# A rotary-embedding kernel: nine transfers on one queue instead of ten, in another order

## The chip, the cores and the metric

One core of a Trainium2 chip runs the kernel. The metric is the device time of one execution in microseconds (us). A profile's span is about 1.7 us shorter than that time (160.1 against 161.85 us in the profiled execution of the kernel before); points in time below count from the start of the span, unless kernel times are meant.

## The reference

The input x is fp32 of shape (16, 512, 16, 64), 33.5 MB. The first 32 of each 64 values are rotated with cosine and sine; the other 32 are copied.

```python
def reference(x, cos, sin):          # cut to what matters; h = 16
    a, b = x[..., 0:16], x[..., 16:32]
    first  = a * cos[..., :16] - b * sin[..., :16]
    second = a * sin[..., :16] + b * cos[..., :16]
    return concatenate([first, second, x[..., 32:]], axis=-1)
```

Every byte of x must come in once and go out once, 67.1 MB in all.

## The kernel before

The data are four tiles of 128 partitions x 64 KB. A partition's part of a tile is 16 rows of 4 KB. Three tiles fit into a ring in SBUF, an on-chip memory, so tile 3 takes the place of tile 0 and cannot be loaded before tile 0 has been stored. All loads and stores are issued by SP (SyncE), on one hardware queue, in program order; VectorE does all arithmetic, in place.

```python
# ... (NS = 3 slots, K = 16 rows, KC = 8, K0 = 4, T = 4 tiles)
    def load(t, lo=0, hi=K):
        nc.sync.dma_start(out=rows(t, lo, hi), in_=xf[t, :, lo * R : hi * R])

    def store(t, lo=0, hi=K):
        nc.sync.dma_start(out=of[t, :, lo * R : hi * R], in_=rows(t, lo, hi))

    nc.gpsimd.dma_start(out=stage[:, 0]..., in_=cosf)      # cut
    nc.gpsimd.dma_start(out=stage[:, 1]..., in_=sinf)      # cut
    load(0, 0, K0)
    load(0, K0, K)
    load(1)
    load(2, 0, KC)
    # ... four VectorE copies spread the tables over 128 partitions
    def rotate(t, lo, hi):
        # ... x1 = first halves of rows lo to hi of tile t; c, s = tables; b_t in PSUM (on-chip too)
        nc.vector.tensor_mul(out=b_t, in0=x1, in1=s)
        nc.vector.tensor_mul(out=x1, in0=x1, in1=c)
        nc.vector.tensor_sub(...)
        nc.vector.tensor_add(...)

    rotate(0, 0, K0)
    rotate(0, K0, (K0 + K) // 2)
    rotate(0, (K0 + K) // 2, K)
    store(0)
    load(2, KC, K)
    load(3)
    for t in range(1, T):
        rotate(t, 0, KC)
        rotate(t, KC, K)
        store(t)
```

So the queue carries: load 0 in 4 and 12 rows, load 1, the first half of load 2, store 0, the second half of load 2, load 3, stores 1, 2, 3. The half load behind store 0 has a purpose: load 3 waits for store 0 to land, and the half load keeps the queue busy meanwhile.

## Time and profile before

| | before |
|---|---|
| kernel time, median of the first 3 runs | 161.82 us (161.75 to 162.03) |
| span of the profiled execution | 160.1 us |
| VectorE (DVE) busy | 110.0 us |
| queue q1, share of 16 engines' span | 97.8% |

From the page of the kernel before: busy time; VectorE's and the DMA engines' share of each of 40 slices, in tenths; the hardware queue (packets, MB, share of the 16 engines' span); and the chain that ended last, by engine (from the last instruction back to what released it, step by step; a q after an engine's name is the part of it that issues and waits).

```profile
DVE 110.0 (69%) x40; POOL 1.3 (1%) x6
...
DVE  0069709999999999999999994799999900000000
...
DMA  6999999699699799899996996996996996996991
...
q1 hardware_dynamic: 1440, 67.11, 97.8%
...
DMA 50%; DVE 28%; DVEq 1%; issue 0%; SPq 0%
```

The row of DMA digits looks ragged (6, 9, 9, 6, ...), but a packet counts in the slice in which it starts, and a 64 KB packet takes 2.4 us against a slice of 4.0 us. The share in the queue's line, 97.8%, is the reading that matters. The trace also keeps a record of each packet: the queue's add up to 156.49 us per engine, and only 156.85 us lie between the first one's start (1.75) and the last one's end (158.60). A 64 KB packet takes 2.418 us in the median, so 16 engines move 16 x 65536 B / 2.418 us = 434 GB/s.

The timeline of the kernel before (start and duration in us; engine, line, operation; output from input; in brackets the idle time before it). SPq lines are issues of transfers; several are merged, with the time from the first issue to the end of the last.

```profile
0.74 1.88 SPq L53 DMA_DIRECT2D ring<-in_x_dram  x4
...
11.94 2.30 DVE L83 TENSOR_TENSOR b_t<-ring,table 128x2048 f32<-128x2048 f32 x1
...
44.14 0.35 SPq L56 DMA_DIRECT2D out_dram<-ring  x1
...
44.53 28.14 SPq L53 DMA_DIRECT2D ring<-in_x_dram  x2
...
72.77 55.64 SPq L56 DMA_DIRECT2D out_dram<-ring  x3
...
125.77 2.28 DVE L88 TENSOR_TENSOR ring<-ring,b_t 128x2048 f32<-128x2048 f32 x1
```

Store 0 is issued at 44.14, while the half load ahead of it in the queue is being moved until 52.2 by the packet records. The last store is issued at about 128.1, while store 2 is being moved until 139.3. No store comes late.

The groups by form, first multiply alone (count, busy us, mean ns, idle before) give what a chunk (the rows of one call of `rotate`) costs:

```profile
L83 DVE TENSOR_TENSOR b_t<-ring,table 128x4096 f32<-128x4096 f32 x6 | 26.6, 4433 | 3.5 <-DMA ring<-in_x_dram 3.3
...
L83 DVE TENSOR_TENSOR b_t<-ring,table 128x3072 f32<-128x3072 f32 x2 | 6.7, 3367 | 4.7 <-DMA ring<-in_x_dram 4.7
...
L83 DVE TENSOR_TENSOR b_t<-ring,table 128x2048 f32<-128x2048 f32 x1 | 2.3, 2301 | 0.0
```

Eight, six and four rows take 4.43, 3.37 and 2.30 us: 0.53 us for each row and 0.17 us over.

### The profile page before, as it was taken

The numbers are of one execution on the slowest core, as the hardware profiler recorded it, in microseconds if no ns is written. First come the engines' busy times: TensorE is split into PE (matmuls) and PEld (weight loads), VectorE is DVE, ScalarE is ACT, GpSimd is POOL, SyncE is SP. The second block draws the span as 40 slices with busy tenths as digits, with TensorE's granted clock in tenths as the row PEclk, the third lists the DMA queues.
The fourth block names the chain that finished last, engine by engine and source line by source line (L and its number), as shares of the span: only waits on it lengthen the run. The fifth ranks groups of instructions, "written<-read, shape, count | busy, mean of one in ns | idle before, by whom it ended". The sixth has DMA issues, their size and how long they took to land.

```text
span 160.1 us, 109 instructions
## 1 busy us (share of the span) xinstructions
DVE 110.0 (69%) x40; POOL 1.3 (1%) x6
## 2 busy tenths in 40 slices
DVE  0069709999999999999999994799999900000000
POOL 3000000000000000000000000000000000000000
DMA  6999999699699799899996996996996996996991
GB/s 197 385 504 454 393 459 524 262 524 491 295 401 581 328 524 409 377 393 418 483 540 295 491 524 262 524 524 262 524 524 262 524 524 262 524 491 295 524 459 66
DMA packets 1504, 67.24 MB, mean 420 GB/s; under 512 B 192, under 2 KB 192, under 8 KB 224
## 3 DMA queue, kind: packets, MB, share of 16 engines
q1 hardware_dynamic: 1440, 67.11, 97.8%
q0 software_dynamic: 64, 0.13, 0.2%
HBM read 33.69 MB, written 33.55 MB: 420 GB/s over the span
## 4 chain that ended last, share of the span: by engine, by line
DMA 50%; DVE 28%; DVEq 1%; issue 0%; SPq 0%
DMA ring<-in_x_dram 32%; DMA out_dram<-ring 18%; DVE b_t L83 10%; DVE ring L84 10%; DVE ring L85 5%; DVE ring L88 3%; DVEq L127 1%; SPq L53 0%; DVEq L83 0%
## 5 line engine op out<-in xcount | busy, mean ns | idle before, releaser
L83 DVE TENSOR_TENSOR b_t<-ring,table 128x4096 f32<-128x4096 f32 (+2 forms) x9 | 35.6, 3959 | 8.2 <-DMA ring<-in_x_dram 8.0
L84 DVE TENSOR_TENSOR ring<-ring,table 128x4096 f32<-128x4096 f32 (+2 forms) x9 | 35.6, 3950 | 0.3
L85 DVE TENSOR_TENSOR ring<-ring,b_t 128x2048 f32<-128x2048 f32 (+2 forms) x9 | 18.4, 2049 | 0.3
L88 DVE TENSOR_TENSOR ring<-ring,b_t 128x2048 f32<-128x2048 f32 (+2 forms) x9 | 18.4, 2042 | 0.0
L67 DVE COPY table<-stage 32x1024 f32<-32x1024 f32 x4 | 2.7, 684 | 9.2 <-DMA stage<-in_sin_dram 9.1
L58 POOL DMA_DIRECT2D stage<-in_cos_dram x1 | 0.6, 631 | 0.8 <-PEq L127 0.8
L59 POOL DMA_DIRECT2D stage<-in_sin_dram x1 | 0.5, 498 | 0.0
L116 POOL MEMSET const-bfloat16-1.0<- 128x1 bf16 x1 | 0.1, 102 | 0.0
L116 POOL MEMSET const-float32-0.0<- 128x1 f32 x1 | 0.1, 99 | 0.2 <-issue 0.2
L116 POOL MEMSET const-float32-1.0<- 128x1 f32 x1 | 0.1, 99 | 0.0
L116 POOL MEMSET const-uint8-127<- 128x1 uint8 x1 | 0.1, 99 | 0.0
## 6 DMA issues: line engine op xcount, KB each, us to landing
ring<-in_x_dram SPq DMA_DIRECT2D x2, 4096.0 KB, 43.9
ring<-in_x_dram SPq DMA_DIRECT2D x1, 6144.0 KB, 22.4
ring<-in_x_dram SPq DMA_DIRECT2D x1, 2048.0 KB, 8.5
stage<-in_cos_dram POOLq DMA_DIRECT2D x1, 64.0 KB, 6.0
stage<-in_sin_dram POOLq DMA_DIRECT2D x1, 64.0 KB, 7.2
out_dram<-ring SPq DMA_DIRECT2D x4, 36.4
ring<-in_x_dram SPq DMA_DIRECT2D x2, 35.0
```

The lines of the kernel that those rows point to most:

```text
L58: nc.gpsimd.dma_start(out=stage[:, 0].rearrange("p k j -> p (k j)"), in_=cosf)
L59: nc.gpsimd.dma_start(out=stage[:, 1].rearrange("p k j -> p (k j)"), in_=sinf)
L67: nc.vector.tensor_copy(out=table[r * PB : (r + 1) * PB].rearrange("p t k c j -> p (t k) c j"), in_=stage.rearrange("p t k j -> p (t k) j" ...
L83: nc.vector.tensor_mul(out=b_t, in0=x1, in1=s)
L84: nc.vector.tensor_mul(out=x1, in0=x1, in1=c)
L85: nc.vector.tensor_sub(out=x1[:, :, :, 0:Q], in0=x1[:, :, :, 0:Q], in1=b_t[:, :, :, Q:HF])
L88: nc.vector.tensor_add(out=x1[:, :, :, Q:HF], in0=x1[:, :, :, Q:HF], in1=b_t[:, :, :, 0:Q])
L116: nc = _bacc.Bacc("TRN2", target_bir_lowering=False, num_devices=1)
L127: with _tile.TileContext(nc) as tc:
```

## The change

The intent, as far as the code tells it, is fewer and larger transfers: three whole loads at once, stores 0 and 1 back to back (store 1 now covers the time in which load 3 waits for store 0), and only the last load in parts, so that its rotation can begin before all of it is there.

```diff
-    K0 = K // 4
+    KA = 7
...
-    load(0, 0, K0)
-    load(0, K0, K)
+    load(0)
     load(1)
-    load(2, 0, KC)
+    load(2)
...
-    rotate(0, 0, K0)
-    rotate(0, K0, (K0 + K) // 2)
-    rotate(0, (K0 + K) // 2, K)
-    store(0)
-    load(2, KC, K)
-    load(3)
-    for t in range(1, T):
+    for t in range(NS - 1):
         rotate(t, 0, KC)
         rotate(t, KC, K)
+        store(t)
+    load(NS, 0, KA)
+    load(NS, KA, K)
+    for t in range(NS - 1, T):
+        cuts = [0, KC, K] if t < NS else [0, KA, (KA + K) // 2, K]
+        for lo, hi in zip(cuts, cuts[1:]):
+            rotate(t, lo, hi)
         store(t)
```

More of the change, by code (lines that the diff above doesn't have):

```diff
@@ L76, in rotate @@
     def rotate(t, lo, hi):
-        n = hi - lo
         x1 = ring[:, t % NS, lo:hi, :, 0:HF]
-        c = C[:, lo:hi].unsqueeze(2).to_broadcast((P, n, H, HF))
-        s = Sn[:, lo:hi].unsqueeze(2).to_broadcast((P, n, H, HF))
+        c = C[:, lo:hi].unsqueeze(2).to_broadcast((P, hi - lo, H, HF))
+        s = Sn[:, lo:hi].unsqueeze(2).to_broadcast((P, hi - lo, H, HF))
         b_full = b_pool.tile([P, KC, H, HF], fp32, name="b_t")
-        b_t = b_full[:, 0:n]
+        b_t = b_full[:, 0 : hi - lo]
         nc.vector.tensor_mul(out=b_t, in0=x1, in1=s)
```

## The prediction

Slack, here and below, is the time from a transfer being ready to the end of the work ahead of it.

> Times count from the start of the span.
>
> **What bounds the kernel now.** The one DMA queue. The page's queue part puts q1 at 97.8% of 16 engines' span, with 67.11 MB. The trace's packet records agree: the queue's packets add up to 156.5 us per engine, and the first packet's start to the last one's end is 156.85 us. A 64 KB packet takes 2.418 us, load or store: 16 x 65536 B / 2.418 us = 434 GB/s. The Trainium skill, "DMA: Bandwidth & Descriptors", section "Where 436 GB/s comes from", gives 435.2 GB/s as the ceiling of the 16 ports; this trace agrees. VectorE is busy 110.0 us (69%), not the bound. The chain of waits looks mixed (DMA 50%, DVE 28%), but its DVE pieces run while the queue is full: store 0 is issued at 44.1, and the last early load lands at 52.6.
>
> **What the change does.** Bytes are the same. Ten transfers become nine, packets 1440 become 1296 (128 rows and 16 completions each). I estimate 0.1 us saved in all, as a packet costs a few ns over its bytes. Start-up (first packets 1.0 to 1.5 us against 0.61 later) and the table loads stay. The queue's floor is the same; the question is whether the new order lets it run dry.
>
> **Does it?** Chunk times from the groups by form: four instructions of 8 rows 13.45 us, 6 rows 10.25, 4 rows 7.05; so I estimate 7 rows 11.85, 5 rows 8.65. A whole tile takes 19.33 us of queue.
> - Tile 0 now arrives whole at about 23.6 (as its second part does now); the first chunk starts 11.7 us later. Rotations 0, 1, 2 end at 50.5, 77.4, 104.3.
> - Queue: load 2 ends at 61.8, store 0 (issued 50.5) at 81.1, store 1 (issued 77.4) at 100.4. Slack 11.3 and 3.7 us.
> - Load 3's parts wait for store 0 to land (about 81.9), 18 us ahead of their turn. They end at 108.9 and 119.8.
> - Store 2 is issued at 104.3 and runs to 139.1.
> - Rotation 3: 7 rows 109.4 to 121.3, 4 rows to 128.3, 5 rows to 137.0. Store 3 is issued at 137.0; issue to first packet was 1.0 us at start-up; packets stand ready by 138.3, and the engines finish store 2 at 138.5 to 139.1. Slack 0.3 to 1 us: tight, but enough.
> - The table loads take turns with the queue packet by packet; behind 64 KB packets they land at about 15 instead of 9.1 (estimate), and the copies (2.8 us) end near 18, before tile 0 arrives.
>
> So almost nothing of the change lies on the critical path: 0.1 us gained from fewer packets, 0 to 0.5 us at risk before the last store.
>
> **Predicted: 161.75 us**, 8 in 10 between 161.4 and 162.4. Faster by over 2%: 0.01; within 2%: 0.97; slower by over 2%: 0.02.
>
> **What would show it.** q1 with 1296 packets and about 98%; DVE idle until 23.6 (with a wait for the table to near 15) and about 5 us before the 7-row chunk; store 3 issued near 137; DVE done 9 us later than now; GB/s flat near 420 to the end.
>
> **What would make it wrong.** A rotation or landing over 1 us late delays store 3 and opens a gap one for one, as nothing else is queued. Less likely: two stores back to back, or load-store switches, running at another rate than 434 GB/s; the table landing after 20.

## The result, and the profile after

| | before | after |
|---|---|---|
| kernel time, median of 6 runs | 161.80 us (161.75 to 162.16) | 161.97 us (161.85 to 162.25) |
| span of the profiled execution | 160.1 us | 160.3 us |
| last work of VectorE ends | 128.1 | 137.2 |
| first packet starts, last packet ends | 1.75, 158.60 | 1.74, 158.91 |
| queue's packets, sum per engine | 156.49 us | 156.22 us |

The ratio is 1.0008, with a 95% interval of 0.9995 to 1.002: the same. Ratios here are the mean time of one kernel's fast runs over that of the other's fast runs of the same rounds, so they are not quite the ratio of the medians quoted.

The same parts of the page, after:

```profile
DVE 110.0 (69%) x40; POOL 1.3 (1%) x6
...
DVE  0000609999999999999999999906999999200000
...
DMA  7969699699699699799899997999996996996990
...
q1 hardware_dynamic: 1296, 67.11, 97.5%
...
DMA 51%; DVE 32%; issue 2%; DVEq 1%
```

VectorE starts two slices later and ends between two and three slices later, and its busy time is the same. There are 144 packets fewer. The DMA row is as full as before.

The timeline after:

```profile
16.60 2.78 DVE L66 COPY table<-stage 32x1024 f32<-32x1024 f32 x4 [16.60 <-DMA stage<-in_sin_dram]
23.85 4.43 DVE L81 TENSOR_TENSOR b_t<-ring,table 128x4096 f32<-128x4096 f32 x1 [4.47 <-DMA ring<-in_x_dram]
...
50.74 27.23 SPq L56 DMA_DIRECT2D out_dram<-ring  x2
...
81.85 1.29 SPq L53 DMA_DIRECT2D ring<-in_x_dram  x2
...
104.51 33.08 SPq L56 DMA_DIRECT2D out_dram<-ring  x2
109.72 3.90 DVE L81 TENSOR_TENSOR b_t<-ring,table 128x3584 f32<-128x3584 f32 x1 [5.23 <-DMA ring<-in_x_dram]
...
121.56 2.30 DVE L81 TENSOR_TENSOR b_t<-ring,table 128x2048 f32<-128x2048 f32 x1
...
128.60 2.83 DVE L81 TENSOR_TENSOR b_t<-ring,table 128x2560 f32<-128x2560 f32 x1
```

A narrower window of the same timeline splits the merged issues and shows the last store alone:

```profile
135.74 1.48 DVE L86 TENSOR_TENSOR ring<-ring,b_t 128x1280 f32<-128x1280 f32 x1
137.25 0.34 SPq L56 DMA_DIRECT2D out_dram<-ring  x1
```

The first rotation starts at 23.85 instead of 11.94, and the last store is issued at 137.25 instead of 128.1. Both delays are nine to twelve microseconds long, and neither reaches the end. By the packet records the 16 engines finish store 2 between 138.7 and 139.6, and store 3's packets follow at once.

The Trainium skill, "HBM Reference", section "Specifications (TRN2)", says that a core streaming alone measures well above its share of the memory, about 425 GB/s, bounded by its 16 DMA engines. Both profiles agree: they show 420 GB/s over the whole span, edges included.

### The profile page after: what moved, and what is told of

It is laid out like the page before. It is cut to its first block, busy times and chain, and to the rows that moved or that the text cites. A ratio compares the mean times of both kernels' runs of the same rounds, so it can differ in the third digit from the quotient of the medians.

```text
span 160.3 us, 108 instructions
## 1 busy us (share of the span) xinstructions
DVE 110.0 (69%) x40; POOL 1.3 (1%) x6
## 4 chain that ended last, share of the span: by engine, by line
DMA 51%; DVE 32%; issue 2%; DVEq 1%
DMA ring<-in_x_dram 32%; DMA out_dram<-ring 19%; DVE b_t L81 11%; DVE ring L82 11%; DVE ring L86 5%; DVE ring L83 4%; DVEq L126 1%; DVEq L81 0%
## 5 line engine op out<-in xcount | busy, mean ns | idle before, releaser
L81 DVE TENSOR_TENSOR b_t<-ring,table 128x4096 f32<-128x4096 f32 (+3 forms) x9 | 35.6, 3959 | 9.9 <-DMA ring<-in_x_dram 9.7
L82 DVE TENSOR_TENSOR ring<-ring,table 128x4096 f32<-128x4096 f32 (+3 forms) x9 | 35.6, 3950 | 0.3
L83 DVE TENSOR_TENSOR ring<-ring,b_t 128x2048 f32<-128x2048 f32 (+3 forms) x9 | 18.4, 2049 | 0.3
L86 DVE TENSOR_TENSOR ring<-ring,b_t 128x2048 f32<-128x2048 f32 (+3 forms) x9 | 18.4, 2042 | 0.0
L66 DVE COPY table<-stage 32x1024 f32<-32x1024 f32 x4 | 2.7, 684 | 16.6 <-DMA stage<-in_sin_dram 16.6
```

The lines of the kernel that those rows point to most:

```text
L66: nc.vector.tensor_copy(out=table[r * PB : (r + 1) * PB].rearrange("p t k c j -> p (t k) c j"), in_=stage.rearrange("p t k j -> p (t k) j" ...
L83: nc.vector.tensor_sub(out=x1[:, :, :, 0:Q], in0=x1[:, :, :, 0:Q], in1=b_t[:, :, :, Q:HF])
L86: nc.vector.tensor_add(out=x1[:, :, :, Q:HF], in0=x1[:, :, :, Q:HF], in1=b_t[:, :, :, 0:Q])
```

## The experiments

Twelve kernels ran, in four groups; each group shares runs of the kernel before on the same chip (medians 162.14, 162.18, 161.92 and 162.03 us), and each ratio is to those. The *queue theory* says: the one queue bounds both kernels, and a delay on VectorE costs time only where it lets the queue run dry. It has several rivals: VectorE's pieces in the chain are really on the path; a transfer has a fixed cost; the table's landing matters. All loads and stores are on one queue in every kernel here. So these runs do not separate the queue from the 16 engines that it fills: a second queue for the loads or the stores was not tried.

The losses of e6, e9 and e11 are under 2%, but their intervals lie well above 1.

### e1: most of VectorE's work taken out

```diff
-        nc.vector.tensor_mul(out=b_t, in0=x1, in1=s)
         nc.vector.tensor_mul(out=x1, in0=x1, in1=c)
-        nc.vector.tensor_sub(...)
-        nc.vector.tensor_add(...)
```

> The changed kernel with three of the four VectorE instructions of each chunk taken out (result wrong on purpose), so VectorE falls from 110 to about 38 us; every transfer stays. Queue theory (the one DMA queue bounds both kernels and only waits that let it run dry cost time): 161.9 us, 161.6 to 162.2. Rival, the chain read at its word (VectorE 32% of the span, 51 us, lies on the path): two thirds of that goes, about 128 us.

Measured: 161.98 us (161.92 to 162.21), ratio 0.9994 (0.9979 to 1.0009); the result is wrong, as meant. From its page:

```profile
DVE 37.9 (24%) x13; POOL 1.3 (1%) x6
...
q1 hardware_dynamic: 1296, 67.11, 97.7%
...
DMA 69%; DVE 7%; DVEq 2%; SPq 0%; issue 0%
```

72 us of VectorE's work are gone and the time is the same. The chain's VectorE share fell from 32% to 7%, and nothing was gained: the chain shows one way back from the end, here through a store's release, not the way that binds. The rival is out.

### e4: the transfers in halves

Every whole load and store of the changed kernel is cut in two, 16 transfers in place of 9.

```diff
-    load(0)
+    load(0, 0, KC)
+    load(0, KC, K)
     ... (the same for loads 1 and 2)
-        store(t)
+        store(t, 0, KC)
+        store(t, KC, K)
```

> The changed kernel with every whole load and store in two halves: 16 transfers in place of 9. Queue theory: a transfer costs its packets' few ns; 161.9 us, 161.6 to 162.3. [...]

Measured: 162.06 us (161.92 to 162.3), ratio 0.9999 (0.9986 to 1.0011).

```profile
q1 hardware_dynamic: 2304, 67.11, 97.8%
```

Seven transfers and 1008 packets more cost nothing that can be seen in the time. (In the one trace the packets add up to 156.98 us per engine, 0.76 more than in the changed kernel, and the last packet ends 0.33 later: about 0.1 us a transfer by the sums, an estimate.) The Trainium skill, "DMA: Bandwidth & Descriptors", section "Anatomy of one DMA", gives a fixed cost of about 2.0 us per DMA, fitted on the software path, and puts most of it down to completion. It does not add up on this queue, which always has a next transfer waiting: seven times 2.0 us (an estimate from that page's figure) would have been 14 us. So the one transfer that the change saves could not be worth 2 us either.

### e2, e3, e5: more work for VectorE in three places

One multiply of 7 rows, 3.9 us, whose result is not used, stands after rotation 2 (e2), 3 (e3) or 1 (e5) of the changed kernel.

```diff
             rotate(t, lo, hi)
+        if t == 2:          # e3: t == 3; e5: t == 1, in the first loop
+            pad(t)          # b_t[:, 0:7] = x1 rows 0 to 7 of tile t, times sin
         store(t)
```

> The changed kernel with one more multiply of 7 rows (3.9 us of VectorE, result unchanged) after rotation 2, where VectorE stands idle 5.2 us before load 3's first part lands. Queue theory: no cost, 161.97 us, within 0.3. Rival, VectorE's work is on the path: up to 3.9 us more, 165.9.

> The same 3.9 us multiply after rotation 3, ahead of the last store. Queue theory: store 3 is issued at 141.2 instead of 137.25; its packets come 1.0 us later, the engines end store 2 at 138.7 to 139.6, so a gap of 2.6 to 3.5 us opens, perhaps with up to 0.6 us of start-up: 164.5 to 166.1 us, centre 165.3. Rival (any VectorE work adds): 165.9, but then e2 must show it too.

> The changed kernel with one more multiply of 7 rows (3.9 us) after rotation 1. Queue theory: store 1 is issued at 81.55 in place of 77.63, its packets come 1.0 us later at 82.55, the engines end store 0 at 80.7 to 81.3: a gap of 1.2 to 1.9 us, perhaps with 0.6 us of start-up, and everything after shifts by it: 163.1 to 164.6 us, centre 163.7. Rival (any VectorE work adds): 165.9.

Measured: e2 162.32 us (ratio 1.0012, 0.9999 to 1.0026), e3 162.35 us (1.0017, 1.0003 to 1.0032), e5 162.24 us (1.0008, 0.9992 to 1.0024). The e2 median lies 0.05 us outside what was expected in absolute terms, and the interval of e3 just leaves out 1. But in these three kernels the time is 2.0 to 2.1 us longer than the span, against 1.7 to 1.85 in every kernel without the extra multiply: about 0.3 us of their time lies outside the span, and its cause is not known. Their spans are those of the kernel before. For e3 and e5 the expectation failed, and the timeline of e3 shows why:

```profile
137.73 0.34 SPq L56 DMA_DIRECT2D out_dram<-ring  x1
137.74 3.90 DVE L92 TENSOR_TENSOR b_t<-ring,table 128x3584 f32<-128x3584 f32 x1
```

The store did not wait for the extra multiply, since it does not read what the multiply writes; the fault was in the experiment. In e5 likewise store 1 went out at 77.42, as in the changed kernel (77.63). Only rotation 2 came 3.9 us later, and store 2 with it, at 108.25; the queue had load 3 to move until 120. So e5 shows that a delay of 3.9 us is absorbed between store 1 and store 2. In e2 store 2 was not delayed either (issued at 104.26): the multiply only filled VectorE's wait for load 3, which fell from 5.23 to 1.56 us. e3 shows nothing on its question, which e11 puts again. From the timelines of e5 and then of e2:

```profile
77.42 0.34 SPq L56 DMA_DIRECT2D out_dram<-ring  x1
...
108.25 0.34 SPq L56 DMA_DIRECT2D out_dram<-ring  x1
```

```profile
109.72 3.90 DVE L81 TENSOR_TENSOR b_t<-ring,table 128x3584 f32<-128x3584 f32 x1 [1.56 <-DMA ring<-in_x_dram]
```

### e6, e7, e8: how the last load is cut

```diff
-    KA = 7
+    KA = 4                  # e6; e7: KA = 8
```

```diff
-    load(NS, 0, KA)         # e8: the last load whole
-    load(NS, KA, K)
+    load(NS)
...
-        cuts = [0, KC, K] if t < NS else [0, KA, (KA + K) // 2, K]
+        cuts = [0, KC, K]
```

> The changed kernel with the last load cut 4 and 12 rows in place of 7 and 9. The second part lands at 120.5 as before, 12 rows then take 20.5 us, store 3 is issued at 141.2. Queue theory: the same as one more multiply before the last store, 164.5 to 166.1 us, centre 165.3. Rival (VectorE's work or the number of transfers sets the time, neither of which changes): 162.0.

> The changed kernel with the last load cut 8 and 8. The first part lands 1.2 us later, store 3 is issued at about 138.5, its packets at 139.5 against engines free at 138.7 to 139.6. Queue theory: 0 to 0.9 us more, 162.0 to 162.9, centre 162.4. Rival (no change of work or transfers): 162.0.

> The changed kernel with the last load whole, rotated as 8 and 8 rows: one transfer fewer. It lands at 120.5, 26.9 us of rotation follow, store 3 is issued at 147.6, its packets at 148.6. Queue theory: a gap of 9.0 to 9.9 us, perhaps with 0.6 us of start-up: 171.0 to 172.5 us, centre 171.7. [...]

| cut of load 3 | store 3 issued | engines end store 2 | all engines idle | kernel time | ratio |
|---|---|---|---|---|---|
| 7 and 9 (the change) | 137.25 | 138.7 to 139.6 | none | 161.97 us | 1.0008 (0.9995 to 1.002) |
| 8 and 8 (e7) | 138.37 | 138.7 to 139.3 | none | 162.07 us | 1.0000 (0.9983 to 1.0016) |
| 4 and 12 (e6) | 141.25 | 138.9 to 139.5 | 2.56 us | 164.69 us | 1.0164 (1.0146 to 1.0182) |
| whole (e8) | 147.74 | 139.1 to 139.8 | 8.78 us | 171.09 us | 1.0573 (1.053 to 1.0616) |

(The ends and the idle time are from the packet records.) The last store in the timelines of e7, e6 and e8:

```profile
138.37 0.34 SPq L56 DMA_DIRECT2D out_dram<-ring  x1
```

```profile
141.25 0.34 SPq L56 DMA_DIRECT2D out_dram<-ring  x1
```

```profile
147.74 0.33 SPq L56 DMA_DIRECT2D out_dram<-ring  x1
```

Windows of e6 and then of e8, from 136 to 148 (us, VectorE busy, GpSimd busy, granted clock, DMA share, GB/s); a packet counts where it starts:

```profile
136.00:139.00 3.00, 2.96 (x2) 0.00 (x0) 1.00 0.81 350
139.00:142.00 3.00, 2.23 (x2) 0.00 (x0) 1.00 0.00 0
142.00:145.00 3.00, 0.00 (x0) 0.00 (x0) 1.00 1.63 699
```

```profile
136.00:139.00 3.00, 2.96 (x2) 0.00 (x0) 1.00 0.81 350
139.00:142.00 3.00, 3.00 (x1) 0.00 (x0) 1.00 0.00 0
142.00:145.00 3.00, 2.97 (x2) 0.00 (x0) 1.00 0.00 0
145.00:148.00 3.00, 2.72 (x2) 0.00 (x0) 1.00 0.00 0
```

In the empty windows no packet starts, while VectorE still rotates tile 3. The queue's share of the span falls to 96.1% (e6) and 92.6% (e8). The loss in kernel time, about 2.6 and 9 us, is the idle time. e8 has one transfer and 144 packets fewer than the changed kernel and is the slowest of all: the count of transfers is not what matters. e7 came out below the centre of its expectation. Its store's packets start at about 139.3, when most engines have stood idle for a few tenths but the slowest is only just done; and it is the slowest that ends the kernel. After it, the engines' ends lie 0.24 us apart, against 0.87 in the changed kernel.

### e11: e3 repaired

```diff
         for lo, hi in zip(cuts, cuts[1:]):
+            if t == 3 and hi == K:
+                pad(t)
             rotate(t, lo, hi)
```

> The repair of e3, whose multiply came after the last chunk, where store 3 does not wait for it: the same 7-row multiply (3.9 us) now stands in front of the last chunk of rotation 3. Queue theory: store 3 is issued at 141.2, as in e6, and the time is e6's 164.7 us, 164.3 to 165.2. Rival (VectorE's extra work never matters, or e6's loss came from the sizes of its two loads and not from the late store): 162.0 to 162.4.

Measured: 165.00 us (164.83 to 165.13), ratio 1.0186 (1.0171 to 1.0201). The timeline of e11:

```profile
128.46 3.90 DVE L92 TENSOR_TENSOR b_t<-ring,table 128x3584 f32<-128x3584 f32 x1
132.40 2.83 DVE L81 TENSOR_TENSOR b_t<-ring,table 128x2560 f32<-128x2560 f32 x1
...
141.04 0.34 SPq L56 DMA_DIRECT2D out_dram<-ring  x1
```

The same 3.9 us of VectorE cost nothing after rotation 2 and about 3 us in front of the last chunk. With the loads cut as in the change, the late store alone makes the loss: all engines stood idle for 2.44 us (packet records), and about 0.3 us of the rest lies outside the span, as in e2, e3 and e5. e6 and e11 issue it at nearly the same moment, by different means, and take nearly the same time.

### e9 and e12: the first load whole, in the order of before

e9 does one step of the change alone, in the kernel before. e12 adds a larger first part of load 2.

```diff
-    load(0, 0, K0)
-    load(0, K0, K)
+    load(0)
     load(1)
-    load(2, 0, KC)
+    load(2, 0, K - K0)      # e12 alone; e9 keeps load(2, 0, KC)
...
-    rotate(0, 0, K0)
-    rotate(0, K0, (K0 + K) // 2)
-    rotate(0, (K0 + K) // 2, K)
+    rotate(0, 0, KC)
+    rotate(0, KC, K)
     store(0)
-    load(2, KC, K)
+    load(2, K - K0, K)      # e12 alone; e9 keeps load(2, KC, K)
```

> The kernel before with its first load whole (rotated as 8 and 8 rows), nothing else changed: the change's first step without its other steps. Rotation 0 ends and store 0 is issued at about 50.7, its packets at 51.7, the engines end the half load of tile 2 at 51.7 to 52.5. Queue theory: at the edge, 0 to 0.6 us more, 161.8 to 162.6, centre 162.1. Rival (the first load's early start is worth the 11.7 us that VectorE starts earlier): about 173.

> e9 again (the kernel before with its first load whole), but load 2 is cut 12 and 4 rows in place of 8 and 8, so that 4.8 us more of loads are queued when store 0 is issued at 50.4. If e9's 2.3 us came of store 0 being issued at the last moment: 161.9 us, 161.6 to 162.4. If they came of the whole first load itself or of anything else in that order, such as slow packets wherever loads and stores change over: about 164.

Measured: e9 164.17 us (163.89 to 164.76), ratio 1.0150 (1.0126 to 1.0174); e12 162.01 us (161.74 to 162.65), ratio 1.0006 (0.9987 to 1.0025).

The chain by engine, of e9 and then of e12, cannot tell them apart:

```profile
DVE 61%; DMA 14%; issue 4%; DVEq 1%
```

```profile
DVE 61%; DMA 14%; issue 5%; DVEq 1%
```

e9 lost over 2 us where 0 to 0.6 were expected, and not as expected: by the packet records no gap opened at store 0, which was issued at 50.37 and whose packets followed load 2's first half at 51.4 to 52.0. Instead, packets themselves were slow, on all 16 engines at once, in two places. These are all the rows after 16 us whose mean excess is over 50 ns (a row is 16 packets, about one per engine; excess is over the usual 2.418 us for 64 KB, 1.213 us for 32 KB, 1.818 us for 48 KB):

```
            mean start us   KB   mean excess ns   largest ns   where
before          50.7        32         59            221       last of load 2's first half
before          97.9        64         58            290       last of load 3
e9              68.7        64        644           1106       last of store 0
e9              71.8        32        370           1180       first of load 2's second half
e9              98.9        64        954           1107       last of load 3
e12             54.8        48        165            590       last of load 2's first part
```

The packets' sum per engine is 158.16 us in e9 and 156.29 in e12. Both places are changes between store and load; in the other kernels the slowest packet at such a change was between nothing and 0.6 us over. e9 was profiled once, but all five of its runs are slow, by their spans too (162.1 to 163.0 us). e12 removes the loss, so the whole first load by itself does not cost it. That more work queued behind it is the remedy is not shown. And why a store issued 1 us ahead of its turn is followed by slow packets 18 and 48 us later is not settled: e12 changes the timing at store 0 and the sizes of load 2's parts together.

### e10: the tables on another queue

```diff
-    nc.gpsimd.dma_start(out=stage[:, 0]..., in_=cosf)
-    nc.gpsimd.dma_start(out=stage[:, 1]..., in_=sinf)
+    nc.scalar.dma_start(out=stage[:, 0]..., in_=cosf)
+    nc.scalar.dma_start(out=stage[:, 1]..., in_=sinf)
```

> The changed kernel with the two table loads issued from the scalar engine's hardware queue in place of GpSimd. Queue theory: the bytes and packets stay nearly the same, the table lands earlier than 16.6 but nothing waits for it: 161.7 us, 161.2 to 162.1; if the tables' packets are what spreads the engines' ends (0.87 us in the changed kernel against 0.54), the spread falls and with it up to 0.3 us. Rival (the table's later landing costs time): 155 to 158.

Measured: 162.02 us (161.93 to 162.42), ratio 1.0010 (0.9995 to 1.0024). The expectation of an earlier table failed; from the groups of e10:

```profile
L66 DVE COPY table<-stage 32x1024 f32<-32x1024 f32 x4 | 2.7, 683 | 18.6 <-DMA stage<-in_sin_dram 18.6
```

The table lands at 18.6, later than the 16.6 of the changed kernel and the 9.1 of before, and still no time is lost, because tile 0's own packets end only at 22.9. The queue lines of e10 and then of the changed kernel show why it is later:

```profile
q10 hardware_dynamic: 96, 0.13, 0.2%
```

```profile
q0 software_dynamic: 64, 0.13, 0.2%
```

On this queue the tables are cut into 96 packets in place of 64, so each engine takes six turns for them in place of four. Between two turns it moves a 64 KB packet of tile 0: by the packet records the six turns begin at 4.7, 7.2, 9.8, 12.3, 14.9 and 17.5 us, the four of the changed kernel at 7.1, 9.9, 12.3 and 15.2. The spread of the engines' ends did not fall (0.94 us). The Trainium skill, "DMA: Bandwidth & Descriptors", section "Issuing engines are not separate DMA queues", says that transfers of all issuers run on the same 16 engines and interleave. This run agrees: the table's packets lie between those of the loads' queue, about 2.5 us apart.

No kernel tried here beats the two. e4 matches them and has more room than the change: its last store is in halves, the first issued at 128.90, when the first engine to end store 2 does so at 139.2, and the second at 137.54, when the first to end the first half does so at 148.8 (packet records). By these numbers and the 0.85 us from issue to first packet, either could come some 9 us later: an estimate, which no run tried.

## Why the prediction was right

The predicted time was 161.75 us (161.4 to 162.4), the measured one 161.97.

- **What binds.** "The one DMA queue", with the 16 engines that it fills: shown by e1 (72 us less of VectorE, ratio 0.9994) from one side, by e6, e8 and e11 from the other, where idle engines appear as lost time.
- **What one transfer fewer saves.** "0.1 us saved in all": nothing that can be seen. The sum of the packets fell by 0.27 us per engine, but the slowest engine ended 0.3 us later. e4 shows that even seven transfers more are not seen.
- **The schedule.** Rotations 0, 1, 2 were to end at 50.5, 77.4 and 104.3; the stores were issued at 50.74, 77.63 and 104.51. The chunks of rotation 3 were to end at 121.3, 128.3 and 137.0; the later two start at 121.56 and 128.60, and store 3 was issued at 137.25. VectorE waited 5.23 us ahead of the 7-row chunk, as predicted. The sums of chunk times held to about 0.3 us over the whole kernel, those of transfer times to about 0.5 (store 2 was to end at 139.1 and ended at 139.6).
- **The table.** Predicted to land at 15, it came at 16.6; with 4.47 us to spare, the miss cost nothing.
- **The slack before the last store.** "0.3 to 1 us" was a little small. e7 issues store 3 1.1 us later and loses nothing that can be seen. Two reasons show: from issue to first packet took about 0.85 us (e6: 141.25 to 142.10), not the 1.0 of the start; and the slowest engine, not the first one done, ends the kernel.
- **"One for one" beyond the slack.** e6, e11 and e8 issue the store 4.0, 3.8 and 10.5 us later than the change, and all engines stand idle for 2.56, 2.44 and 8.78 us. That is one for one after the first 1.4 to 1.7 us. The changed kernel's own records give the same: a store issued at 137.25 has packets ready at about 138.1, and the slowest engine ends store 2 at 139.6.

Where the change put its risk is now plain. The whole first load takes 11.9 us from VectorE's head start; the whole third load pays for it with more queued work ahead of store 0. Store 1 behind store 0 covers the landing of store 0. The price is a last load at the very end of the loads, and the 7 and 9 rows are what keeps that from costing: without the cut the kernel loses 9 us (e8).

The prediction named one risk, as less likely, that it had no way to reckon: changes between load and store at another rate. In e9 packets there do become slow although the queue is full. Had the change done its first step alone, the same reckoning would have been wrong by 2 us. The changed kernel was spared (its slowest row of packets after 16 us is 0.09 us over), and as the cause in e9 is open, that part of the success is luck.

## What to carry to other kernels

When one queue is full from the first packet to the last, reckon a reordering by one question at each transfer: is it issued before the work ahead of it runs out, and by how much? Durations of chunks and transfers read from one trace answer that to a few tenths of a microsecond, and the chain that ended last does not (VectorE's share of it was 28%, 32%, 7% and 61% in kernels of the same time). Spend the slack knowingly: this change trades slack of about 10 us before the last store for 1 to 1.5, and gains nothing for it. When you delay a store by extra work in an experiment, check that the store really waits for that work.

## What the Trainium skill lacked or had wrong

- "DMA: Bandwidth & Descriptors", section "Where 436 GB/s comes from": its sentence that for transfers between HBM and SBUF the memory's side, about 358 GB/s, binds does not hold for a core that runs alone. Here 64 KB packets moved at 434 GB/s and the whole span averaged 420. (The lines around it on the page, and "HBM Reference", section "Specifications (TRN2)", do make this exception.)
- The same page, section "Anatomy of one DMA": the fixed cost of about 2.0 us is not said to vanish where the next transfer is already queued. Seven transfers more on a full queue cost nothing visible (e4, ratio 0.9999).
- The same page, section "Queues, rings and completion order": it tells that an engine takes turns between queues by packets, and a turn's length in descriptors, but not in time. Beside 64 KB rows each turn of the loads' queue is 2.4 us, and a 64 KB table load landed at 16.6 (software queue) or 18.6 (hardware queue, e10) in place of 9.1.
- No page has it: packets can become slow at changes between store and load though the queue is full, by about 1 us on each of the 16 engines, twice in e9, which made it 1.5% slower; the cause is open.
